# Seven block products instead of eight in the down projection of a feed-forward network

## The chip, the cores and the metric

The kernel is one program on one core of a Trainium2 chip. The metric is the device time of one execution in microseconds (us). The kernel before takes 3278.21 us, the median of three runs from 3277.07 to 3279.9.

The core has TensorE (PE, matmuls), VectorE (DVE), ScalarE (ACT), GpSimd (POOL) and SyncE (SP, whose queue issues the DMAs). Operands lie in SBUF; matmuls write banks of PSUM, 128 partitions by 512 float32.

## The reference

Two transformer blocks on 1024 tokens of width 1024, one after the other, in float32. They hold three feed-forward networks (FFN) of hidden width 2816; these are what matters here:

```python
        up = dwconv3(h @ w_up[l], conv_w[l], conv_b[l])      # first block
        gate, val = jnp.split(up, 2, axis=-1)
        y = (jax.nn.gelu(gate) * val) @ w_down[l]
        x = x + gt_f * rms_norm(y, g_post_ffn[l])
...
def swiglu(x, w_gu, w_down):                                  # second block, twice
    g, u = jnp.split(x @ w_gu, 2, axis=-1)
    return (jax.nn.silu(g) * u) @ w_down
```

The rest (state space and Fourier mixers, two attentions, projections, a last gated layer) is outside the change.

## The kernel before

**Precision.** Every float32 operand is split into a high part (`F32R`, cast by ScalarE, L58) and the remainder (VectorE subtracts, L59). One product is then three matmuls, high x high, high x low, low x high (`mm3`, L96 to L98). `split` is used all over the kernel.

**Up stage of an FFN.** The hidden width is cut into `nff` = 22 tiles of 128. The activation lies transposed and split in `hT`, four tiles with tags `hh` and `hl` of two places each. After two tiles done plainly, the loop over `j` computes each tile with seven block products (`prod`, L296) on sums S1 to S3 of the activation's blocks, which fill the three places of tag `S`. Every finished hidden tile, 128 x 1024, is stored to DRAM (`hidden[j]`, L320 or L246).

**Down stage.** The output, 8 row tiles x 1024, accumulates in SBUF in `yacc` (two places of tag `S`). `load(j)` brings the hidden tile (L357) and 128 rows of `w_down` (L361) into two `raw` places, of which there are three, and splits them: the hidden tile into two places of `b4` (twelve), the weights into `wh` and `wl` (four each). `down` takes two tiles at once: for each of 16 banks six matmuls, then one addition of the bank into `yacc` by VectorE (L377), or for the first pair a copy by ScalarE (L375). Nine such pairs cover 18 tiles. The last four tiles are loaded together and done in one call with 12 matmuls for each bank; behind each row tile `finish` normalises it, adds the residual and prepares the next layer.

**What sets the order.** The program text gives dependencies; a scheduler of the framework then lays out each engine's queue, which runs strictly in that order, and waits between engines are semaphores. Tiles come from pools with a fixed number of places for each tag; a new tile waits until the oldest one's last reader is done. PSUM has six banks under tag `mm` and two under `tp`.

Of the kernel before, what the change touches and what calls it, by code (L numbers as in the profile page):

```python
# [5 lines left out]
F32 = mybir.dt.float32  # L6
F32R = mybir.dt.float32r
I32 = mybir.dt.int32
AF = mybir.ActivationFunctionType
OP = mybir.AluOpType  # L10
PSUM = bass.MemoryType.PSUM
DRAM = bass.MemoryType.DRAM
P = 128
D = 1024
NT = 8
# [4 lines left out]
def f(ap):  # L20
    return ap.bitcast(F32)
# [167 lines left out]
def ffn(k, hT, w_gu, w_down, nff, prep, finish, taps=None, then=None):  # L189
# [5 lines left out]
    nc, v, pool = k.nc, k.nc.vector, k.nc.gpsimd  # L195
    with k.tc.tile_pool(name="ffn", bufs=1) as fp:
        k.places(fp, "b4", 12)
        hidden = k.dr.tile([nff, P, D], F32, name=f"hidden{k.count()}")

        def b4(dt=F32):  # L200
            return fp.tile([P, D], dt, name="b4", tag="b4", bufs=12)

        def big(shape, dt):
            return fp.tile([P] + shape, dt, name="S", tag="S", bufs=3)
# [54 lines left out]
        for a in range(0, 4, 2):  # L259
            c = slice(a, a + 2)  # L260
# [38 lines left out]
        lo, hi = slice(0, 512), slice(512, 1024)  # L299
# [23 lines left out]
        for j in range(2, nff):  # L323
            w = weights(j)
            A, B, C = k.mm(), None, None
# [5 lines left out]
            s, V = b4(), b4()  # L331
            B = k.mm()
# [16 lines left out]
        finish_tile(*prev)  # L349


        ys = [big([4, D], F32) for _ in range(2)]
        yacc = [ys[i // 4][:, i % 4] for i in range(NT)]

        def load(j):
            r = k.raw([P, D])
            nc.sync.dma_start(r, hidden[j])  # L357
            h = b4(F32R), b4(F32R)
            k.split(*h, r)
            r = k.raw([P, D])  # L360
            nc.sync.dma_start(r, w_down[j * P:(j + 1) * P, :])  # L361
            w = k.wide()
            k.split(*w, r)
            return h + w

        def down(ready, first, last):
            for i in range(NT):
                t = slice(i * P, i * P + P)
                for n in range(2):
                    c = slice(n * 512, n * 512 + 512)  # L370
                    po = k.mm()
                    for a, (hh, hl, wh, wl) in enumerate(ready):
                        k.mm3(po, (hh[:, t], hl[:, t]), (wh[:, c], wl[:, c]), a == 0, a == len(ready) - 1)
                    if first:
                        nc.scalar.activation(yacc[i][:, c], po, AF.Copy)  # L375
                    else:
                        v.tensor_tensor(yacc[i][:, c], yacc[i][:, c], po, op=OP.add)  # L377
                if last:
                    finish(fp, i, yacc[i])
                    if i >= 4:  # L380
                        k.flush(2, 1)

        n = nff - 4
        for j in range(0, n, 2):
            down([load(j), load(j + 1)], j == 0, False)
        rows = big([4, D], F32)
        k.rows = [rows[:, a] for a in range(3)]
        k.junk = rows[:, 3]
        prep(fp)
        down([load(j) for j in range(n, nff)], False, True)  # L390
        k.close()
        if then is not None:
            then(fp)
# [10 lines left out]
class Filler:  # L404
# [6 lines left out]
    def add(self, gen):  # L411
        self.jobs.append(gen)
        return gen

    def step(self):
        try:
            return next(self.jobs[0])
        except StopIteration:
            self.jobs.pop(0)
            return 0.0  # L420
# [5 lines left out]
    def finish(self, gen=None):  # L426
        while self.jobs and (gen is None or gen in self.jobs):
            self.step()
# [144 lines left out]
class Mixture:  # L573
# [6 lines left out]
    def put(self, pool, kt, h, src):  # L580
        c = slice(h * 512, h * 512 + 512)
        t = [pool.tile([P, 512], F32R, name=f"mix{a}", tag=f"mix{a}", bufs=2) for a in range(2)]
        self.k.split(t[0], t[1], src)
        for a in range(2):
            self.k.nc.sync.dma_start(self.d[a][kt, :, c], f(t[a]))
# [1283 lines left out]
```

## Time and profile before

| | |
|---|---|
| median of three runs | 3278.21 us |
| the profiled execution | 3276.33 us |
| its span on the core | 3274.3 us |
| TensorE busy | 3088.8 us, 94% |
| VectorE busy | 2133.0 us, 65% |
| ScalarE busy | 1274.7 us, 39% |
| GpSimd busy | 788.9 us, 24% |
| mean granted TensorE clock | 0.976 |

The profile is one execution. Busy times of engines overlap, so they don't add up to the span. In lists of groups a row gives line, engine, operation, out<-in by the program's names with buffer numbers left out (`b` is `b4`), shapes and count, then busy time and mean ns of one, then the idle time ahead of it and what ended it. A matmul's record is longer than the distance to the next one, since they are pipelined; the pace has to be read from starts.

### The profile page before, as it was taken

To read this page: it belongs to the slowest core of one execution; us is meant where nothing else is said; L and a number is where in the kernel's file an instruction comes from. 1 tells how busy PE (TensorE), PEld (TensorE's weight loads), DVE (VectorE), ACT (ScalarE), POOL (GpSimd) and SP (SyncE) were. 2 spreads that over 40 slices of the span, in tenths; PEclk is the share of its full clock that TensorE was granted. 3 is DMA by queue.
4 is the path that set the end of the run, shared out by engine and by line. 5 is a ranking of instruction groups with operands and counts; after the bars stand their busy time and mean duration, and the time that the engine had idled before them with its cause. 6 is when DMAs were issued, how large, how long until landed. Compare 5 with 4: busy or idle time off the path is not lost. (4 is left out here: it accounts for less than half of the span.)

```text
span 3274.3 us, 40844 instructions
## 1 busy us (share of the span) xinstructions
PE 3088.8 (94%) x15362; PEld 2523.1 (77%) x15362; DVE 2133.0 (65%) x3648; ACT 1274.7 (39%) x1975; POOL 788.9 (24%) x903
## 2 busy tenths in 40 slices
PE   5989988899999998999999999999998999999988
PEld 2766767788887878888888878777787788888867
DVE  7766588766666678444446686667677444456686
ACT  3335633444543124333341145446623333341132
POOL 3468525322220014322300020000014222200022
PEclk8999999999999999999999999999998999999999
DMA  7573553122224232222242342111631222242344
GB/s 207 172 223 118 159 175 118 65 90 78 84 90 142 92 129 71 89 78 86 88 141 92 96 142 82 46 45 68 212 129 52 84 77 90 84 148 94 98 144 154
DMA packets 282104, 362.87 MB, mean 111 GB/s; under 512 B 35559, under 2 KB 208871, under 8 KB 281906
## 3 DMA queue, kind: packets, MB, share of 16 engines
q1 hardware_dynamic: 273442, 345.73, 32.7%
q10 hardware_dynamic: 6576, 9.00, 0.8%
q0 software_dynamic: 1888, 5.53, 0.6%
q8 instruction: 121, 1.98, 0.2%
q14 instruction: 77, 0.63, 0.1%
HBM read 274.84 MB, written 91.66 MB: 112 GB/s over the span
## 5 line engine op out<-in xcount | busy, mean ns | idle before, releaser
L296 PE MATMUL mm<-S,wh 128*128 128x512 f32 x1440 | 443.5, 389 | 2.0 <-ACT b L328 2.0
L96 PE MATMUL mm<-wh,b 128*128 128x512 f32 x1056 | 414.3, 393 | 4.0 <-ACT b L58 4.0
L97 PE MATMUL mm<-wl,b 128*128 128x512 f32 x1056 | 413.4, 392 | 0.0
L98 PE MATMUL mm<-wh,b 128*128 128x512 f32 x1056 | 411.9, 391 | 0.0
L377 DVE TENSOR_TENSOR S<-S,mm 128x512 f32<-128x512 f32 x432 | 289.1, 684 | 128.9 <-PE mm L98 128.0
L59 DVE TENSOR_TENSOR wl<-raw,wh 128x1024 fp32r<-128x1024 f32 x242 | 320.3, 1325 | 60.6 <-ACT wh L58 60.4
L58 ACT ACTIVATE wh<-raw 128x1024 fp32r<-128x1024 f32 x244 | 253.4, 1053 | 261.7 <-PE mm L296 140.2
L296 PEld LDWEIGHTS mm<-S,wh 128*128 128x128 f32 x1440 | 270.2, 188 | 58.6 <-ACT b L328 2.4
L96 PE MATMUL mm<-hh,wh 128*128 128x256 f32 (+1 forms) x880 | 300.1, 341 | 15.5 <-ACT hh L58 15.3
L97 PE MATMUL mm<-hl,wh 128*128 128x256 f32 (+1 forms) x880 | 298.9, 340 | 3.5 <-DVE hl L59 3.5
L98 PE MATMUL mm<-hh,wl 128*128 128x256 f32 (+1 forms) x880 | 297.0, 338 | 4.6 <-DVE wl L59 4.6
L296 PE MATMUL mm<-hh,wh 128*128 128x512 f32 x720 | 284.0, 395 | 13.6 <-ACT wh L58 9.8
L296 PE MATMUL mm<-hh,wl 128*128 128x512 f32 x720 | 283.5, 394 | 9.8 <-DVE wl L59 9.8
L296 PE MATMUL mm<-hl,wh 128*128 128x512 f32 x720 | 283.1, 393 | 0.0
L296 PE MATMUL mm<-S,wl 128*128 128x512 f32 x720 | 280.2, 389 | 0.0
L151 POOL TENSOR_TENSOR S<-S 128x1024 f32<-128x1024 f32 x24 | 58.9, 2453 | 802.6 <-ACT S L145 785.9
L343 DVE TENSOR_TENSOR b<-mm,b 128x512 f32<-128x512 f32 x60 | 41.5, 692 | 319.4 <-PE mm L296 314.1
L96 PEld LDWEIGHTS mm<-wh,b 128*128 128x128 f32 x1056 | 199.9, 189 | 45.6 <-ACT b L58 4.5
L97 PEld LDWEIGHTS mm<-wl,b 128*128 128x128 f32 x1056 | 200.0, 189 | 42.5 <-DVE wl L59 0.9
L98 PEld LDWEIGHTS mm<-wh,b 128*128 128x128 f32 x1056 | 199.2, 189 | 42.7 <-DVE b L59 1.2
L58 ACT ACTIVATE b<-raw 128x1024 fp32r<-128x1024 f32 x66 | 69.6, 1059 | 402.1 <-PE mm L97 247.6
L286 POOL TENSOR_TENSOR b<-raw,b 128x512 f32<-128x512 f32 x60 | 79.7, 1329 | 573.8 <-DVE wl L59 573.8
(385 smaller groups left out, 6454.0 us busy)
## 6 DMA issues: line engine op xcount, KB each, us to landing
raw<-in_ffn_w_gu SPq DMA_DIRECT2D x88, 512.0 KB, 3.8
hidden<-b SPq DMA_DIRECT2D x66, 512.0 KB, 2.6
raw<-hidden SPq DMA_DIRECT2D x66, 512.0 KB, 4.5
raw<-in_w_ada SPq DMA_DIRECT2D x48, 512.0 KB, 3.7
raw<-in_w_up SPq DMA_DIRECT2D x44, 512.0 KB, 3.8
raw<-in_ffn_w_down SPq DMA_DIRECT2D x44, 512.0 KB, 4.3
x<-tmp SPq DMA_DIRECT2D x40, 512.0 KB, 2.6
tmp<-x SPq DMA_DIRECT2D x40, 512.0 KB, 5.5
```

Of the source, the lines that this page charges most:

```text
L58: self.nc.scalar.activation(hi, src, AF.Copy)
L59: (eng or self.nc.vector).tensor_tensor(lo, src, f(hi), op=OP.subtract)
L96: mm(out, a[0], b[0], start=start, stop=False)
L97: mm(out, a[0], b[1], start=False, stop=False)
L98: mm(out, a[1], b[0], start=False, stop=stop)
L151: self.nc.gpsimd.tensor_tensor(y, y, row, op=OP.mult)
L286: pool.tensor_tensor(T[:, up], rg[:, dn], T[:, dn], op=OP.subtract)
L296: nc.tensor.matmul(ps, w[y][:, a], x[z][:, a], start=start and a == 0 and n == 0, stop=a == 3 and n == 2, skip_group_check=True)
L343: v.tensor_tensor(V[:, lo], C, X[:, lo], op=OP.add)
L377: v.tensor_tensor(yacc[i][:, c], yacc[i][:, c], po, op=OP.add)
```

## The change

The nine pairs become three groups of three pairs. In a pair the hidden tiles are the operand A (tile j gives A's first half of the inner dimension, tile j+1 the second; tokens 0 to 511 and 512 to 1023 are its other halves), and the weights are B, with two halves of 512 columns. The four blocks of the output come from seven block products, numbered 1 to 7, in the order 1, 2, 5, 3, 6, 7, 4. Each product is done for all three pairs of the group, in four banks, one for 128 tokens: nine matmuls in a bank. Products 1, 6, 7 and 4 accumulate in the same four banks, 5 and 3 share a bank too, and 2 has banks of its own; after each product a bank is added to that part of `yacc` which it belongs to (`collect`). The operands of 1, 2 and 7 are blocks as they are; those of 5, 3, 6 and 4 need sums, which GpSimd makes in place, 24 of 128 x 512 for a group.

`Group` loads six hidden tiles and six weight tiles: a1 into the three `raw` places, b1 into one place of `S`, a2 and b2 into `b4`. `put` splits the operands of one product, in 512 columns each. The split blocks go where the activation lay (`hh`, `hl`, two places each) and into `wh` and `wl`. `step()` prepares the next product's operands ahead in the program text. In the first group, a part of `yacc` is first written by a copy on ScalarE. The last four tiles stay as they were.

```diff
--- before.py
+++ after.py
@@ -349,9 +349,6 @@
...
-        ys = [big([4, D], F32) for _ in range(2)]
-        yacc = [ys[i // 4][:, i % 4] for i in range(NT)]
...
-        def down(ready, first, last):
-            for i in range(NT):
-                t = slice(i * P, i * P + P)
-                for n in range(2):
-                    c = slice(n * 512, n * 512 + 512)
-                    po = k.mm()
-                    for a, (hh, hl, wh, wl) in enumerate(ready):
-                        k.mm3(po, (hh[:, t], hl[:, t]), (wh[:, c], wl[:, c]), a == 0, a == len(ready) - 1)
-                    if first:
-                        nc.scalar.activation(yacc[i][:, c], po, AF.Copy)
...
+        def wblock():
+            tag = ("wh", "wl")[turn["w"] % 2]
+            turn["w"] += 1
+            return k.g.tile([P, D], F32R, name=tag, tag=tag, bufs=k.wbufs)
+        def ablocks():
+            tag = ("hh", "hl")[turn["a"] % 2]
+            turn["a"] += 1
+            return k.g.tile([P, 8, 512], F32R, name=tag, tag=tag, bufs=2).rearrange("p (a b) c -> p a b c", a=4)
+        def bank():
+            turn["s"] += 1
+            if turn["s"] % 2:
+                return k.mm()
+            return k.ps.tile([P, 4, P], F32, name="tp", tag="tp", bufs=2).rearrange("p a b -> p (a b)")
+        class Group:
+            def __init__(self, js):
+                self.js, g = js, len(js)
+                self.b1 = big([4, D], F32)
+                self.a1, self.a2, self.b2 = [], [], []
+                for m, j in enumerate(js):
+                    self.a1.append(k.raw([P, D]))
+                    nc.sync.dma_start(self.a1[m], hidden[j])
+                    nc.sync.dma_start(self.b1[:, m], w_down[j * P:(j + 1) * P, :])
+                for m, j in enumerate(js):
+                    self.a2.append(b4())
+                    nc.sync.dma_start(self.a2[m], hidden[j + 1])
+                    self.b2.append(b4())
+                    nc.sync.dma_start(self.b2[m], w_down[(j + 1) * P:(j + 2) * P, :])
+                self.blocks = {}
+            def put(self, name, a, b):
+                A = ablocks()
+                r = []
+                for m in range(len(self.js)):
+                    x, y = a(m), b(m)
+                    k.split(A[:, m, 0], A[:, m, 1], x)
+                    if m < 2:
+                        B = wblock()
+                        B = B[:, lo], B[:, hi]
                     else:
-                        v.tensor_tensor(yacc[i][:, c], yacc[i][:, c], po, op=OP.add)
-                if last:
-                    finish(fp, i, yacc[i])
-                    if i >= 4:
-                        k.flush(2, 1)
-        n = nff - 4
-        for j in range(0, n, 2):
-            down([load(j), load(j + 1)], j == 0, False)
+                        B = A[:, 3, 0], A[:, 3, 1]
+                    k.split(*B, y)
+                    r.append(((A[:, m, 0], A[:, m, 1]), B))
+                self.blocks[name] = r
+            def prep(self, name):
+                a1, a2, b1, b2 = self.a1, self.a2, [self.b1[:, m] for m in range(len(self.js))], self.b2
+                add = lambda o, x, y: pool.tensor_tensor(o, x, y, op=OP.add)
+                sub = lambda o, x, y: pool.tensor_tensor(o, x, y, op=OP.subtract)
+                if name == 1:
+                    self.put(1, lambda m: a1[m][:, lo], lambda m: b1[m][:, lo])
+                elif name == 2:
+                    self.put(2, lambda m: a2[m][:, lo], lambda m: b2[m][:, lo])
+                elif name == 5:
+                    def s1(m):
+                        t = self.b1[:, 3, lo if m % 2 == 0 else hi]
+                        add(t, a1[m][:, hi], a2[m][:, hi])
+                        return t
+                    def t1(m):
+                        sub(b1[m][:, lo], b1[m][:, hi], b1[m][:, lo])
+                        return b1[m][:, lo]
+                    self.put(5, s1, t1)
+                elif name == 3:
+                    def s4(m):
+                        sub(a1[m][:, hi], a1[m][:, lo], a1[m][:, hi])
+                        sub(a1[m][:, lo], a2[m][:, hi], a1[m][:, hi])
+                        sub(a2[m][:, lo], a2[m][:, lo], a1[m][:, lo])
+                        return a2[m][:, lo]
+                    self.put(3, s4, lambda m: b2[m][:, hi])
+                elif name == 6:
+                    def t2(m):
+                        sub(b1[m][:, hi], b2[m][:, hi], b1[m][:, hi])
+                        sub(b2[m][:, hi], b2[m][:, hi], b1[m][:, lo])
+                        return b2[m][:, hi]
+                    self.put(6, lambda m: a1[m][:, lo], t2)
...
+            def run(self, first, step):
+                def product(po, name, i, start):
+                    t = slice(i * P, i * P + P)
+                    bs = self.blocks[name]
+                    for m, ((ah, al), (bh, bl)) in enumerate(bs):
+                        for z, (x, y) in enumerate(((ah, bh), (ah, bl), (al, bh))):
+                            nc.tensor.matmul(po, x[:, t], y, start=start and m == 0 and z == 0,
+                                             stop=m == len(bs) - 1 and z == 2, skip_group_check=True)
+                def collect(po, i, h, c, new):
+                    y = yacc[i + 4 * h][:, c]
+                    if first and new:
+                        nc.scalar.activation(y, po, AF.Copy)
+                    else:
+                        v.tensor_tensor(y, y, po, op=OP.add)
+                step()
+                U = [k.mm() for _ in range(4)]
+                for i in range(4):
+                    product(U[i], 1, i, True)
+                    collect(U[i], i, 0, lo, True)
+                step()
+                for i in range(4):
+                    po = bank()
+                    product(po, 2, i, True)
+                    collect(po, i, 0, lo, False)
+                step()
+                step()
+                for i in range(4):
+                    po = bank()
+                    product(po, 5, i, True)
+                    collect(po, i, 1, hi, True)
+                    product(po, 3, i, False)
+                    collect(po, i, 0, hi, True)
+                for name, h, c, new in ((6, 0, hi, False), (7, 1, hi, False), (4, 1, lo, True)):
+                    step()
+                    for i in range(4):
+                        product(U[i], name, i, False)
+                        collect(U[i], i, h, c, new)
+        order = (1, 2, 5, 3, 6, 7, 4)
+        groups = [range(j, j + 6, 2) for j in range(0, n, 6)]
+        def preps():
+            for js in groups:
+                gr = Group(js)
+                made.append(gr)
+                for name in order:
+                    gr.prep(name)
+                    yield
+        made = []
+        ahead = preps()
+        next(ahead)
+        ys = [big([4, D], F32) for _ in range(2)]
+        yacc = [ys[i // 4][:, i % 4] for i in range(NT)]
+        for a in range(len(groups)):
+            made[a].run(a == 0, lambda: next(ahead, None))
...
+        ready = [load(j) for j in range(n, nff)]
+        for i in range(NT):
+            t = slice(i * P, i * P + P)
+            for c in (lo, hi):
+                po = k.mm()
+                for a, (hh, hl, wh, wl) in enumerate(ready):
+                    k.mm3(po, (hh[:, t], hl[:, t]), (wh[:, c], wl[:, c]), a == 0, a == len(ready) - 1)
+                v.tensor_tensor(yacc[i][:, c], yacc[i][:, c], po, op=OP.add)
+            finish(fp, i, yacc[i])
...
```

**VectorE, amid the first FFN's down stage.** Before, at the beginning of the third pair (L377 adds a bank to `yacc`, L59 is the subtraction of a split, `b4` and `wl` the low parts of hidden tile and weights):

```order
L377 TENSOR_TENSOR S_8392<-S_8392,mm_8722 128x512 [waits DVE_49,PE_49]
L59 TENSOR_TENSOR wl_8859<-raw_8856,wh_8858 128x1024 [waits DMAHW4_49,Activation_49]
L377 TENSOR_TENSOR S_8392<-S_8392,mm_8730 128x512 [waits DVE_49,PE_49]
L377 TENSOR_TENSOR S_8392<-S_8392,mm_8738 128x512 [waits DVE_49,PE_49]
L59 TENSOR_TENSOR wl_8871<-raw_8868,wh_8870 128x1024 [waits DMAHW6_49,Activation_49]
L377 TENSOR_TENSOR S_8392<-S_8392,mm_8746 128x512 [waits DVE_49,PE_49]
L377 TENSOR_TENSOR S_8392<-S_8392,mm_8754 128x512 [waits DVE_49,PE_49]
L59 TENSOR_TENSOR b4_9017<-raw_9014,b4_9016 128x1024 [waits DMAHW1_49,Activation_49]
```

Now, in the second group, from the first addition of product 1 (L479 is `collect`, tags `hh`, `hl`, `wh` hold the split blocks):

```order
L479 TENSOR_TENSOR S_8429<-S_8429,mm_8889 128x512 [waits PE_49]
L59 TENSOR_TENSOR hh_8998<-b4_8815,hh_8998 128x512 [waits Activation_49]
L59 TENSOR_TENSOR hh_8998<-b4_8817,hh_8998 128x512 [waits Activation_49]
L479 TENSOR_TENSOR S_8429<-S_8429,mm_8890 128x512 [waits PE_49]
L479 TENSOR_TENSOR S_8429<-S_8429,mm_8891 128x512 [waits PE_49]
L59 TENSOR_TENSOR wh_9027<-b4_8809,wh_9027 128x512 [waits Activation_49]
L59 TENSOR_TENSOR wl_9034<-b4_8813,wl_9034 128x512 [waits Activation_49]
L479 TENSOR_TENSOR S_8429<-S_8429,mm_8892 128x512 [waits PE_49]
L59 TENSOR_TENSOR hl_9022<-raw_8798,hl_9022 128x512 [waits Activation_49]
L59 TENSOR_TENSOR hl_9022<-raw_8801,hl_9022 128x512 [waits Activation_49]
L479 TENSOR_TENSOR S_8429<-S_8429,mm_8954 128x512 [waits DVE_49,PE_49]
```

Additions and splits still alternate, but a split has 512 columns instead of 1024, and there are more of them: over a group 42 splits and 28 additions, where three pairs had 12 and 48.

**GpSimd, same group.** Its queue had nothing here in the kernel before. Now it begins like this (L423 an S1 sum into the free fourth part of b1, L424 the differences, in place on a1 in `raw`, b1 in `S`, a2 and b2 in `b4`):

```order
L423 TENSOR_TENSOR S_8797<-raw_8798,b4_8807 128x512 [waits DMAHW7_49,DMAHW1_49,DVE_49]
L424 TENSOR_TENSOR raw_8798<-raw_8798 128x512 [waits Pool_49]
L423 TENSOR_TENSOR S_8797<-raw_8801,b4_8811 128x512 [waits DMAHW3_49,DMAHW0_49]
L424 TENSOR_TENSOR raw_8801<-raw_8801 128x512 [waits Pool_49]
L424 TENSOR_TENSOR S_8797<-S_8797 128x512 [waits DMAHW1_49,DVE_49]
L424 TENSOR_TENSOR S_8797<-b4_8809,S_8797 128x512 [waits DMAHW2_49,Pool_49]
L424 TENSOR_TENSOR raw_8798<-b4_8807,raw_8798 128x512 [waits DVE_49]
L424 TENSOR_TENSOR raw_8801<-b4_8811,raw_8801 128x512 [waits DVE_49]
L424 TENSOR_TENSOR S_8797<-S_8797 128x512 [waits DMAHW2_49,DVE_49]
L424 TENSOR_TENSOR S_8797<-b4_8813,S_8797 128x512 [waits DMAHW4_49,Pool_49]
```

Differences in place wait for the split that reads the old value (`DVE_49`) or for the sum just made (`Pool_49`).

**TensorE, products 5 and 3 of the same group.** Before, every bank was six matmuls and then free for VectorE, and the next bank was another one:

```order
L96 MATMUL mm_8810<-wh_8706,b4_8700 128x512 [waits DVE_49]
L97 MATMUL mm_8810<-wl_8707,b4_8700 128x512
L98 MATMUL mm_8810<-wh_8706,b4_8701 128x512
L96 MATMUL mm_8810<-wh_8718,b4_8712 128x512
L97 MATMUL mm_8810<-wl_8719,b4_8712 128x512
L98 MATMUL mm_8810<-wh_8718,b4_8713 128x512
L96 MATMUL mm_8818<-wh_8706,b4_8700 128x512 [waits DVE_49]
```

Now one bank takes product 5 (operand `hl_8933`), is collected, and then takes product 3 (`hh_8998`):

```order
L471 MATMUL mm_9043<-wh_8938,hl_8933 128x512 [waits DVE_49]
L471 MATMUL mm_9043<-wh_8938,hl_8933 128x512 x2
L471 MATMUL mm_9043<-wl_8945,hl_8933 128x512 x3
L471 MATMUL mm_9043<-hl_8933 128x512 x3
L471 MATMUL tp_9064<-wh_8938,hl_8933 128x512 [waits DVE_49]
L471 MATMUL tp_9064<-wh_8938,hl_8933 128x512 x2
L471 MATMUL tp_9064<-wl_8945,hl_8933 128x512 x3
L471 MATMUL mm_9043<-wh_9004,hh_8998 128x512 [waits DVE_49,Activation_49]
L471 MATMUL mm_9043<-wh_9004,hh_8998 128x512 x2
L471 MATMUL mm_9043<-wl_9012,hh_8998 128x512 [waits Activation_49]
L471 MATMUL mm_9043<-wl_9012,hh_8998 128x512 x2
L471 MATMUL mm_9043<-hh_8998 128x512 [waits Activation_49]
```

Between the last matmul of product 5 in bank `mm_9043` and the first of product 3 the order puts six matmuls of the next bank; the wait for `DVE_49` at product 3's first matmul covers the collection of that bank.

Outside the three down stages the queues of all engines hold the same instructions in the same order as before.

## Rows read from the trace of the kernel before

**Rows 1.** page, span, then busy us (share of span) and instructions per engine
```profile
span 3274.3 us, 40844 instructions
PE 3088.8 (94%) x15362; PEld 2523.1 (77%) x15362; DVE 2133.0 (65%) x3648; ACT 1274.7 (39%) x1975; POOL 788.9 (24%) x903
```

**Rows 2.** stretches: width, busy us (x instructions) per engine, clock, DMA share, GB/s
```profile
core 0: us, PE busy (x) PEld busy (x) DVE busy (x) ACT busy (x) POOL busy (x), PEclk, DMA share, GB/s
980.00:1000.00 20.00, 15.96 (x63) 12.41 (x62) 11.73 (x10) 12.45 (x17) 0.00 (x0) 0.91 0.38 128
1000.00:1020.00 20.00, 20.00 (x89) 16.54 (x89) 11.49 (x14) 11.54 (x16) 0.00 (x0) 1.00 0.74 239
1020.00:1040.00 20.00, 20.00 (x90) 16.57 (x89) 14.93 (x20) 2.96 (x3) 0.00 (x0) 1.00 0.30 93
1680.00:1700.00 20.00, 20.00 (x88) 16.25 (x87) 11.16 (x12) 11.51 (x16) 0.00 (x0) 1.00 0.70 234
2900.00:2920.00 20.00, 20.00 (x89) 16.24 (x88) 10.85 (x11) 11.52 (x15) 0.00 (x0) 1.00 0.60 198
```

**Rows 3.** order of time, ScalarE, second FFN: start us, us, engine, line, [idle <-releaser]
```profile
1704.31 0.60 ACT L375 ACTIVATE S<-mm 128x512 f32<-128x512 f32 x1 [0.76 <-PE mm L98]
1705.67 0.60 ACT L375 ACTIVATE S<-mm 128x512 f32<-128x512 f32 x1 [0.76 <-PE mm L98]
```

**Rows 4.** order of time, VectorE: a split alone, three additions in a row
```profile
961.32 0.68 DVE L59 TENSOR_TENSOR b<-b,b 128x512 fp32r<-128x512 f32 x1
...
1718.37 1.88 DVE L377 TENSOR_TENSOR S<-S,mm 128x512 f32<-128x512 f32 x3
```

**Rows 5.** groups by line: engine, op, shapes, count | busy us, mean ns | idle
```profile
L58 ACT ACTIVATE b<-b 128x512 fp32r<-128x512 f32 x60 | 37.6, 627 | 44.7 <-POOL b L286 44.5
```

**Rows 6.** order of time, GpSimd at 613 us, VectorE idle
```profile
613.35 1.29 POOL L280 TENSOR_TENSOR b<-raw,b 128x512 f32<-128x512 f32 x1
614.59 1.29 POOL L281 TENSOR_TENSOR raw<-raw 128x512 f32<-128x512 f32 x1
```

**Rows 7.** order of time, 1289 to 1296 us, GpSimd, then VectorE
```profile
1289.38 2.16 POOL L280 TENSOR_TENSOR b<-raw,b 128x512 f32<-128x512 f32 x1
1291.49 2.26 POOL L281 TENSOR_TENSOR raw<-raw 128x512 f32<-128x512 f32 x1
...
1292.54 2.30 DVE L265 TENSOR_TENSOR b<-b,b 128x1024 f32<-128x1024 f32 x1
1294.76 1.21 DVE L59 TENSOR_TENSOR S<-b,S 128x1024 fp32r<-128x1024 f32 x1
```

**Rows 8.** order of time, 604 us, GpSimd, then VectorE
```profile
604.83 3.25 POOL L286 TENSOR_TENSOR b<-raw,b 128x512 f32<-128x512 f32 x1 [21.28 <-DVE wl L59]
...
604.60 2.35 DVE L59 TENSOR_TENSOR wl<-raw,wh 128x1024 fp32r<-128x1024 f32 x2
```

**Rows 9.** order of time, 1207 us, GpSimd, then VectorE
```profile
1207.16 2.77 POOL L151 TENSOR_TENSOR S<-S 128x1024 f32<-128x1024 f32 x1 [5.20 <-ACT S L145]
...
1207.84 0.68 DVE L377 TENSOR_TENSOR S<-S,mm 128x512 f32<-128x512 f32 x1
```

**Rows 10.** order of time, TensorE, first FFN, where up ends and down begins
```profile
981.99 0.39 PE L296 MATMUL mm<-hh,b 128*128 128x512 f32 x1
986.42 0.50 PE L96 MATMUL mm<-wh,b 128*128 128x512 f32 x1 [4.04 <-ACT b L58]
...
990.40 0.48 PE L98 MATMUL mm<-wh,b 128*128 128x512 f32 x1
990.72 0.39 PE L96 MATMUL mm<-wh,b 128*128 128x512 f32 x1
```

**Rows 11.** order of time, VectorE, same place: the hidden tile's last multiplication
```profile
990.24 1.22 DVE L319 TENSOR_TENSOR b<-b,b 128x1024 f32<-128x1024 f32 x1
```

**Rows 12.** page, DMA issues: KB each, us to landing
```profile
raw<-hidden SPq DMA_DIRECT2D x66, 512.0 KB, 4.5
```

More of the change, by code (lines that the diff above doesn't have):

```diff
@@ L383, in ffn @@
-        n = nff - 4
-        for j in range(0, n, 2):
-            down([load(j), load(j + 1)], j == 0, False)
+        n = nff - 4
+        lo, hi = slice(0, 512), slice(512, D)
+        turn = {"w": 0, "a": 0, "s": 0}
+        def wblock():
[6 more added lines that the diff above has]
+            return k.g.tile([P, 8, 512], F32R, name=tag, tag=tag, bufs=2).rearrange("p (a b) c -> p a b c", a=4)
@@ new lines, in bank, with t4 @@
+        def bank():
[27 more added lines that the diff above has]
+                        B = B[:, lo], B[:, hi]
+                    else:
+                        B = A[:, 3, 0], A[:, 3, 1]
[32 more added lines that the diff above has]
+                    self.put(6, lambda m: a1[m][:, lo], t2)
+                elif name == 7:
+                    self.put(7, lambda m: a1[m][:, hi], lambda m: b1[m][:, hi])
+                else:
+                    def t4(m):
+                        sub(b2[m][:, lo], b2[m][:, lo], b2[m][:, hi])
+                        return b2[m][:, lo]
+                    self.put(4, lambda m: a2[m][:, hi], t4)
+            def run(self, first, step):
[10 more added lines that the diff above has]
+                        nc.scalar.activation(y, po, AF.Copy)
+                    else:
+                        v.tensor_tensor(y, y, po, op=OP.add)
[22 more added lines that the diff above has]
+                        collect(U[i], i, h, c, new)
@@ L389, in ffn @@
         prep(fp)
-        down([load(j) for j in range(n, nff)], False, True)
+        ready = [load(j) for j in range(n, nff)]
[7 more added lines that the diff above has]
+            finish(fp, i, yacc[i])
+            if i >= 4:
+                k.flush(2, 1)
         k.close()
```

## Prediction

> **What bounds the kernel now.** I read the engines' busy times first, then the busy times by stretch, then the order of instructions in time. TensorE is busy 94% of the span, VectorE 65%, ScalarE 39%, GpSimd 24% [rows 1]. Shares are averages, so the stretches of the down stage count: from 1020 us on each 20 us hold 20.00 us of TensorE at clock 1.00, beside some 14 us of VectorE, 4 us of ScalarE and nothing on GpSimd [rows 2]. The second and third FFN enter the stage without a gap; the first loses time there [rows 2]. So this stage is paid in matmuls, and GpSimd is free in it. The pace: ScalarE copies out one bank per six matmuls, waiting for TensorE each time, and two copies start 1.36 us apart [rows 3]; 1.36/6 = 0.2267 us a matmul.
>
> **The change, part by part.**
>
> *Matmuls removed.* A group of three tile pairs took 3 x 96 = 288 matmuls, 65.3 us. Seven products of four banks of nine matmuls are 252, 57.1 us. Three groups in each of three FFNs: 9 x 36 = 324 fewer, 73.5 us off, if TensorE stays the bound. The last four tiles of each FFN and everything outside the down stage keep their instructions.
>
> *VectorE.* Three pairs had 48 additions into S and 12 splits of 1024 columns. Now a group has 28 additions of 512 columns and 42 splits of 512. Three additions back to back take 1.88 us, so 0.60 us each; a 512-column split takes 0.68 alone [rows 4], and I take 0.60 for it in a row too. 70 x 0.60 = 42.0 us in 57.1. In the first group 16 additions are copies on ScalarE; VectorE has 54 x 0.60 = 32.4 us.
>
> *ScalarE.* 42 casts of 512 columns at 0.627 us [rows 5] are 26.3 us, in a first group 16 copies of 0.60 [rows 3] more, 35.9 us. Both fit under 57.1; no cost where there are tiles to work ahead on, and there are four operand blocks, so that three products, 24 us, can lie prepared.
>
> *GpSimd.* 24 sums of 512 columns per group. Undisturbed they start 1.24 us apart [rows 6]: 29.8 us. That fits too, were it alone. It is not: at 1289 to 1294 us GpSimd's 512-column sums take 2.16 and 2.26 us, and the vector addition of 1024 columns beside them 2.30 instead of 1.21 [rows 7]. They take turns; a collision costs VectorE 1.09 us. At 604.83 it is GpSimd that waits, 3.25 us, while two splits run at full speed [rows 8]. The addition that reads PSUM is spared: 0.68 us inside a GpSimd sum of 2.77 [rows 9]. So the 42 splits, which read two SBUF operands, and the 24 sums exclude each other; the 28 additions from PSUM can hide a sum.
>
> *Time of a group.* Below: were every sum over an addition, 42.0 + 24 x 1.09 - 24 x 0.60 = 53.8 us, and TensorE's 57.1 bounds. Above: nothing hidden, 42.0 + 29.8 = 71.8 us. In the queue additions and splits stand mixed, 28 of 70 are additions, so I let 40% of the collisions be hidden, as if sums came at random: 42.0 + 0.6 x 26.2 = 57.7 us. That is level with TensorE, and two loads that are level do not mesh without loss. Where they touch is the hand-over from product 5 to product 3 in one bank: the order leaves 4 to 6 matmuls (0.9 to 1.4 us) between the end of one and the start of the other, in which the bank must be added up (0.68 us). A split held for 1.09 us ahead of that addition makes it 0.4 to 0.9 us late, and behind it on VectorE stand the next bank's addition and splits. Four hand-overs a group: some 2.3 us. I take 60.0 us for the second and third group, nearest to the random figure, and keep 57.1 and 71.8 as ends. The first group, with 16 additions fewer, has 32.4 + 15.7 = 48.1 us on VectorE and stays TensorE's. Six groups pay 2.9 us each: +17.4 us.
>
> *Start of a stage.* The first group has nothing prepared. Its first product needs b1, which takes a place of the activation's sums S; these are free after their last product, 48 matmuls (10.9 us) before the up stage ends. From then nine loads of 512 KB, 4.7 MB, at the 239 GB/s of the best stretch [rows 2] take 19.7 us, so the last lands 8.8 us after the up stage; product 2 wants it 9.5 us after (one product of 8.2 us, and two thirds of a bank) less 1.3 us for cast and split: late by 0.6 us. At the 128 GB/s of the stretch before it [rows 2] the loads take 36.7 us and are 17 us late. The GpSimd chain is the other clock: the last S1 sum, which product 5 needs 17.7 us after the up stage, stands fourteenth in GpSimd's queue, 17.4 us of sums that may start some 4 us early, longer where splits hold them. In order with it wait the sums of product 3. So between 0 and 17 us; near the rows of 234 to 239 GB/s I take 4 us for the second and third FFN. In the first FFN the vector engine still runs the convolution, and the store of the last hidden tile stands before the last load on SP's queue. There the trace of before already pays: TensorE idles 4.04 us and then starts 11 matmuls in the 4.30 us from 986.42 to 990.72, of which [rows 10] show the first and the last, instead of in 2.49, 5.9 us. The multiplication that ends the tile starts at 990.24 and takes 1.22 us [rows 11], 9.1 us after the up stage's last matmul ended at 982.38 [rows 10]; a load behind that store lands about 4.5 us later [rows 12], 13.6 us, which with 1.3 us is 5.4 us after product 2 wants it. Old and new loss cancel: 0. Together +8 us.
>
> *Elsewhere.* Loads and stores are the same number of bytes. In the later groups the loads of a2 and b2 run ahead, and raw and b1 come free once product 7 is prepared, some 24 us before the next group begins; six loads at 239 GB/s need 13.2 us. No cost. The last four tiles' casts stand among the last group's additions as they did.
>
> *Sum*, on the profiled execution of 3276.33 us (a span of 3274.3 [rows 1] and 2.0 around it): 3276.3 - 73.5 + 17.4 + 8 = 3228.2. The median of the runs lies 1.9 us above that execution: 3230 us.
>
> **A rule to weigh.** The turns in [rows 7] and the wait in [rows 8] show that whoever comes second waits for a whole instruction. The Trainium skill (SBUF — State Buffer, "Who interferes with whom") says the same of a vector instruction with two SBUF inputs against a GpSimd instruction that reads SBUF, calls it an exclusive lock, and leaves the loser to the order of issue; the rows agree. By it nothing but the additions from PSUM could hide a sum, which is the end of 53.8 to 71.8 us already reckoned. Its page "Perfetto Trace Analysis", section "Optimizing Scalar/DVE Operations", goes further: moving work between these two might not help at all. Taken at its word that is rival B below.
>
> **The rivals.**
>
> *A. TensorE stays the bound everywhere.* For it: VectorE has 15 us to spare in a group and prepares three products ahead; two splits in a row can pass a waiting sum [rows 8]. Against: 57.7 us is not below 57.1. Time: 3276.3 - 73.5 + 8 + 1.9 = 3213 us, and with no loss at the starts and the old gap of the first FFN filled some 3199.
>
> *B. The shared port becomes the bound, and the kernel is slower.* The place is VectorE's queue in groups two and three: each sum holds a split, the additions behind it come late, the banks stay full, TensorE waits. At 71.8 us such a group is 6.5 us longer than before; the first group takes 32.4 + 29.8 = 62.2, 3.1 less than before; with 2.7 for the start an FFN gains 12.6 us: 3278.2 + 38 = 3316 us. It decides from about 68 us a group, where 2 x 2.7 equals what the first group, at 57.1, still wins less the start (8.2 - 2.7). TensorE would be busy 80 to 84% there; in the stretch of before with 15.96 of 20 us the granted clock was 0.91 [rows 2], which would add to it. Against: additions and splits are well mixed in the queue, so that nothing hidden is an extreme.
>
> *C. The starts cost what their upper end says.* 17 us in each FFN from late loads or the GpSimd chain, and 60 us a group: 3276.3 - 73.5 + 17.4 + 51 + 1.9 = 3273 us. For it: 12 loads and 24 sums crowd into the first 30 us, and ScalarE's queue mixes product 2's casts with copies that wait for product 1. Against: the up stage's end has the rate of 234 GB/s already in the second FFN [rows 2].
>
> *D. It doesn't do what it says.* 324 matmuls do leave the instruction order, so this has next to no weight.
>
> **How the numbers follow.** Forecast 0.45, A 0.20, C 0.15, B 0.15, the rest 0.05. The forecast's own range is 3213 to 3255. The range down to 3200 takes in A; up to 3285 it takes in C and B's beginning, leaving most of B and a little below A out. What a measurement can tell from no change is about 0.2%, 6.6 us: 3271.7 to 3284.8. Faster than that: the forecast, A, and most of C, 0.77. Within: the rest of C and a mild B, 0.08. Slower: 0.15.
>
> **What would show it.** In the down stage each 252 matmuls should take 57 us in the first group and near 60 in the others, with TensorE 95% busy and clock 1.00. VectorE's splits should show two lengths, 0.68 and up to 1.8 us, GpSimd's sums 1.29 and up to 2.3, the additions from PSUM 0.68 throughout. TensorE's waits should name VectorE's additions at the hand-overs, and loads, splits or casts of product 2 and 5 in the first group. I am wrong if groups two and three run at 57 us (the port is no bound) or above 65 (it is the only bound), or if more than 10 us is idle at a start.

## The result and the profile after

The kernel with the change takes 3308.7 us, the median of four runs (3299.72 to 3314.56), beside 3277.82 us for the kernel before on the same chip. The ratio is 1.0091, interval 1.0067 to 1.0114: 0.9% slower, where 3230 us was forecast and 3285 was the upper end. In the profiled executions the mean granted clock fell from 0.976 to 0.961.

The page of the profiled execution (3314.56 us), the lines that answer to [rows 1]:

```profile
span 3312.8 us, 40565 instructions
PE 3060.1 (92%) x15038; PEld 2479.6 (75%) x15038; DVE 2275.7 (69%) x3738; ACT 1380.9 (42%) x2245; POOL 1129.4 (34%) x1119
```

15038 matmuls instead of 15362 are 324 fewer, as counted. Yet the span is 38.5 us longer (the medians differ by 30.9 us; the profiled execution is the slowest of the four). Next, the stretches of the kernel after, with the columns of [rows 2]. The first nine rows are the nine groups, three for each FFN, each from its first matmul to the next group's first, a third group to the end of its last matmul's record, which is 0.16 us past the start of the next matmul; the width is the second number.

```profile
985.78:1073.62 87.84, 70.08 (x265) 52.93 (x264) 77.89 (x73) 42.40 (x75) 61.76 (x39) 0.88 0.40 148
1073.62:1138.68 65.06, 60.14 (x253) 47.84 (x252) 56.07 (x67) 25.59 (x46) 37.51 (x26) 0.97 0.13 49
1138.68:1200.93 62.25, 58.33 (x254) 47.14 (x253) 49.96 (x66) 21.21 (x31) 12.68 (x8) 1.00 0.41 136
1700.97:1785.82 84.85, 67.03 (x266) 52.00 (x264) 71.10 (x69) 38.48 (x71) 59.49 (x39) 0.88 0.41 146
1785.82:1851.02 65.20, 60.27 (x253) 47.91 (x252) 56.03 (x67) 25.54 (x46) 37.45 (x26) 0.97 0.13 49
1851.02:1914.09 63.07, 59.76 (x254) 48.29 (x253) 49.81 (x66) 21.22 (x31) 12.70 (x8) 0.97 0.41 134
2937.22:3019.16 81.94, 65.41 (x266) 50.82 (x265) 71.59 (x69) 38.48 (x71) 59.80 (x39) 0.90 0.41 150
3019.16:3084.27 65.11, 60.19 (x254) 47.85 (x252) 56.03 (x67) 25.53 (x46) 37.49 (x26) 0.97 0.14 49
3084.27:3146.56 62.29, 58.31 (x254) 47.15 (x253) 49.95 (x66) 21.22 (x31) 12.70 (x8) 1.00 0.39 135
...
1700.00:1720.00 20.00, 13.97 (x59) 10.57 (x58) 20.00 (x14) 7.72 (x14) 19.11 (x12) 0.94 0.76 288
1720.00:1740.00 20.00, 11.98 (x43) 9.13 (x43) 15.75 (x14) 10.27 (x20) 16.69 (x12) 0.72 0.09 36
1740.00:1760.00 20.00, 17.92 (x65) 14.09 (x66) 10.65 (x19) 9.36 (x18) 5.13 (x4) 0.83 0.60 199
1780.00:1800.00 20.00, 20.00 (x90) 16.53 (x89) 19.85 (x19) 8.79 (x16) 16.10 (x10) 1.00 0.00 1
```

Three things are to be seen. First groups are the worst: 82 to 88 us, slower than the 65.3 us of three pairs before. They hold 12 matmuls of the up stage's end besides their 252, so TensorE's own pace would be 57.1 + 12 x 0.2267 = 59.8 us. (The counts in the rows also take in records that overlap an end of the stretch.) Second groups take 65 us and third groups 62 to 63, beside 57.1. And in 1700 to 1720 us VectorE is busy all 20.00 us with only 14 instructions, GpSimd 19.11 with 12: 1.4 and 1.6 us each, for tiles of 512 columns.

VectorE, then GpSimd, in order of time there (start, duration, engine, line; L59 split, L306 a multiplication of the up stage, L423 and L424 the sums, L479 `collect`), answering to [rows 4, 7]:

```profile
1704.09 1.77 DVE L59 TENSOR_TENSOR wh<-b,wh 128x512 fp32r<-128x512 f32 x1
1705.78 1.78 DVE L59 TENSOR_TENSOR wh<-S,wh 128x512 fp32r<-128x512 f32 x1
1707.48 1.78 DVE L59 TENSOR_TENSOR wh<-b,wh 128x512 fp32r<-128x512 f32 x1
1709.19 1.77 DVE L306 TENSOR_TENSOR b<-b,b 128x512 f32<-128x512 f32 x1
...
1740.54 0.67 DVE L479 TENSOR_TENSOR S<-S,mm 128x512 f32<-128x512 f32 x1
1741.14 0.68 DVE L59 TENSOR_TENSOR wl<-b,wl 128x512 fp32r<-128x512 f32 x1
...
1703.57 1.74 POOL L423 TENSOR_TENSOR S<-raw,b 128x512 f32<-128x512 f32 x1
1705.39 1.62 POOL L424 TENSOR_TENSOR raw<-raw 128x512 f32<-128x512 f32 x1
1707.09 1.62 POOL L424 TENSOR_TENSOR raw<-b,raw 128x512 f32<-128x512 f32 x1
1708.67 1.74 POOL L424 TENSOR_TENSOR S<-b,S 128x512 f32<-128x512 f32 x1
```

Both engines start a new instruction every 1.69 us: one on VectorE and one sum in turn, from 1703.6 us to the end of that stretch. From 1739.9 us, with GpSimd idle, VectorE starts an instruction every 0.60 us again. The split pays the 1.09 us of [rows 7]; the sum pays some 0.4 us. This is the exclusive lock that the Trainium skill describes (SBUF — State Buffer, "Who interferes with whom"); the rows agree, but for an overlap of 0.15 us: alone the two would take 0.60 + 1.24 = 1.84 us.

What TensorE waited for in that first group ([idle <-releaser]), and two waits of the second group:

```profile
1716.09 0.73 PE L471 MATMUL mm<-wl,hl 128*128 128x512 f32 x2 [1.99 <-DVE wl L59]
1725.85 0.79 PE L471 MATMUL mm<-hl 128*128 128x512 f32 x1 [9.03 <-ACT hl L58]
1728.24 1.22 PE L471 MATMUL mm<-hl 128*128 128x512 f32 x2 [1.60 <-DVE hl L59]
1742.08 1.65 PE L471 MATMUL mm<-wh,hl 128*128 128x512 f32 x3 [2.65 <-ACT S L477]
...
1802.78 0.96 PE L471 MATMUL mm<-wh,hl 128*128 128x512 f32 x3 [0.48 <-DVE S L479]
1808.88 0.93 PE L471 MATMUL mm<-wh,hh 128*128 128x512 f32 x3 [2.40 <-DVE S L479]
```

And ScalarE's queue ahead of the long one:

```profile
1713.84 0.63 ACT L58 ACTIVATE hh<-S 128x512 fp32r<-128x512 f32 x1 [5.09 <-POOL S L423]
...
1724.64 0.63 ACT L58 ACTIVATE hh<-S 128x512 fp32r<-128x512 f32 x1 [8.65 <-POOL S L423]
1725.18 0.61 ACT L58 ACTIVATE hl<-b 128x512 fp32r<-128x512 f32 x1
```

ScalarE stood 8.65 us at a cast of product 5 (operand in `S`, made by an L423 sum), and the cast of product 2 that TensorE wanted (`hl<-b`) stood behind it. After such waits TensorE goes on at the lower of its two levels (1.2 GHz): three matmuls take 1.65 us at 1742.08 instead of the 0.84 of the three at 1737.68, and 1740 to 1760 us holds 65 matmuls at clock 0.83 where the full stretch at 1780 holds 90.

### The profile page after: what moved, and what is told of

Its sections match the earlier page's. It is cut to its first block, busy times and chain, and to the rows that moved or that the text cites. A ratio compares the mean times of both kernels' runs of the same rounds, so it can differ in the third digit from the quotient of the medians.

```text
span 3312.8 us, 40565 instructions
## 1 busy us (share of the span) xinstructions
PE 3060.1 (92%) x15038; PEld 2479.6 (75%) x15038; DVE 2275.7 (69%) x3738; ACT 1380.9 (42%) x2245; POOL 1129.4 (34%) x1119
## 5 line engine op out<-in xcount | busy, mean ns | idle before, releaser
L296 PEld LDWEIGHTS mm<-S,wh 128*128 128x128 f32 x1440 | 271.0, 188 | 58.6 <-ACT b L328 2.4
L58 ACT ACTIVATE wh<-raw 128x1024 fp32r<-128x1024 f32 x190 | 199.2, 1055 | 258.7 <-PE mm L296 141.5
L59 DVE TENSOR_TENSOR wl<-raw,wh 128x1024 fp32r<-128x1024 f32 x188 | 254.8, 1357 | 43.2 <-ACT wh L58 42.9
L151 POOL TENSOR_TENSOR tmp<-tmp,row 128x1024 f32<-128x1024 f32 x16 | 42.3, 2648 | 580.8 <-DMA raw<-in_ffn_w_gu 443.3
L96 PEld LDWEIGHTS mm<-hh,wh 128*128 128x128 f32 x880 | 172.2, 196 | 33.1 <-ACT hh L58 16.8
L98 PEld LDWEIGHTS mm<-hh,wl 128*128 128x128 f32 x880 | 171.7, 195 | 21.7 <-DVE wl L59 5.4
L97 PEld LDWEIGHTS mm<-hl,wh 128*128 128x128 f32 x880 | 172.1, 196 | 18.4 <-DVE hl L59 4.1
L296 PEld LDWEIGHTS mm<-hh,wh 128*128 128x128 f32 x720 | 137.2, 191 | 43.5 <-ACT wh L58 10.4
L296 PEld LDWEIGHTS mm<-hh,wl 128*128 128x128 f32 x720 | 137.1, 190 | 40.5 <-DVE wl L59 11.8
L277 POOL TENSOR_TENSOR b<-raw 128x512 f32<-128x512 f32 x60 | 81.1, 1352 | 232.6 <-DMA raw<-in_ffn_w_gu 108.9
L296 PE MATMUL mm<-hh,b 128*128 128x512 f32 x480 | 157.9, 390 | 1.7 <-DVE b L347 1.7
L296 PEld LDWEIGHTS mm<-hl,wh 128*128 128x128 f32 x720 | 137.2, 191 | 28.5
```

Source lines behind the costliest of these rows:

```text
L58: self.nc.scalar.activation(hi, src, AF.Copy)
L59: (eng or self.nc.vector).tensor_tensor(lo, src, f(hi), op=OP.subtract)
L96: mm(out, a[0], b[0], start=start, stop=False)
L97: mm(out, a[0], b[1], start=False, stop=False)
L98: mm(out, a[1], b[0], start=False, stop=stop)
L151: self.nc.gpsimd.tensor_tensor(y, y, row, op=OP.mult)
```

## The experiments

The leading theory, P, is the port: VectorE's splits and GpSimd's sums exclude each other and both queues are held. Against it stands Q: operands come late because they wait for sums, and in ScalarE's queue for casts that wait for sums, whoever makes the sums and however fast the splits are. A third, late loads, has the trace against it: 1700 to 1720 us moved 288 GB/s, more than any stretch of [rows 2].

All times are medians; the ratio is to the kernel before on the same chip. That kernel took 3277.82 us beside the kernel after, 3281.39 beside e1 to e4 and 3282.4 beside e5 to e7, so differences in us between kernels of different sets are uncertain by up to some 5 us. Width of the three groups in the second FFN, read from the stretches as above:

| kernel | us | ratio (interval) | groups, us |
|---|---|---|---|
| after | 3308.7 | 1.0091 (1.0067 to 1.0114) | 84.8, 65.2, 63.1 |
| e1, no sums | 3205.09 | 0.9769 (0.9754 to 0.9784) | 60.5, 57.6, 58.1 |
| e2, sums nobody waits for | 3315.74 | 1.0108 (1.0093 to 1.0123) | 78.1, 72.9, 58.6 |
| e3, sums on VectorE | 3202.76 | 0.9759 (0.9743 to 0.9776) | 60.7, 57.2, 57.4 |
| e4, casts in another order | 3299.33 | 1.0055 (1.0040 to 1.0070) | 79.6, 65.2, 62.8 |
| e5, first group on VectorE | 3268.87 | 0.9960 (0.9946 to 0.9974) | 68.6, 65.5, 63.0 |
| e6, later groups on VectorE | 3268.42 | 0.9959 (0.9944 to 0.9975) | 79.6, 57.5, 58.8 |
| e7, half on VectorE | 3272.09 | 0.9972 (0.9962 to 0.9982) | 72.8, 61.0, 63.6 |

**e1: no sums.** In `prep` of the kernel after (the other sums likewise):

```diff
-                add = lambda o, x, y: pool.tensor_tensor(o, x, y, op=OP.add)
-                sub = lambda o, x, y: pool.tensor_tensor(o, x, y, op=OP.subtract)
+                side = lambda x, y: None
...
-                        t = self.b1[:, 3, lo if m % 2 == 0 else hi]
-                        add(t, a1[m][:, hi], a2[m][:, hi])
-                        return t
+                        side(a1[m][:, hi], a2[m][:, hi])
+                        return a1[m][:, hi]
```

> The 24 block sums of each group are left out; products 5, 3, 6 and 4 take unsummed blocks. Theory P (port): GpSimd's sums and VectorE's splits exclude each other, and this makes the first group of each stage 82 to 88 us and the others 63 to 65 instead of 57. Then without sums every split takes 0.68 us, the later groups 57 to 58 us, the first 57 to 62, and the time is 3205 to 3220 us. Theory Q (queue): the first group is late because product 2's casts stand in ScalarE's queue behind casts that wait for sums; without sums that goes too, but the later groups stay at 63 to 65: 3240 to 3255 us. Theory R (neither: late loads, 70 small vector instructions, copies out of banks): groups stay as they are, 3290 us or more.

Measured: 3205.09 us, 103.6 less than after. The three groups of the second FFN:

```profile
1657.08:1717.57 60.49, 60.49 (x265) 49.16 (x264) 43.04 (x70) 39.45 (x72) 0.00 (x0) 1.00 0.56 202
1717.57:1775.21 57.64, 57.64 (x254) 46.99 (x253) 43.34 (x70) 24.72 (x44) 0.00 (x0) 1.00 0.15 55
1775.21:1833.26 58.05, 57.89 (x254) 47.22 (x253) 42.28 (x62) 21.01 (x31) 0.00 (x0) 1.00 0.41 145
```

Splits, casts, loads, banks and the program's order are as in the kernel after, and TensorE's only gap here is 0.16 us, in the third group; at the start there is none. In the first FFN its waits in the down stage add up to 1.9 us. So neither the loads nor the 512-column splits nor the hand-over in one bank cost much by themselves; nearly all of the loss comes with the sums. Whether through the port or through waiting for them, e2 tells.

**e2: the same sums, read by nobody.**

```diff
-                add = lambda o, x, y: pool.tensor_tensor(o, x, y, op=OP.add)
-                sub = lambda o, x, y: pool.tensor_tensor(o, x, y, op=OP.subtract)
+                side = lambda x, y: pool.tensor_tensor(self.b1[:, 3, lo], x, y, op=OP.add)
```

and the calls as in e1.

> GpSimd makes the same 24 sums of the same operands, but into a scratch place that nobody reads; the products take unsummed blocks. Theory P: the port is as contended as before, splits beside sums take 1.7 us and the later groups stay at 61 to 65 us; only the chain sum, cast, split is gone from the first group: 3250 to 3285 us. If it is the waiting for sums and not the port (dependency), the time is that of the kernel without sums, 3205 to 3220 us. Theory R: 3290 us or more.

Measured: 3315.74 us, no better than after. The groups of the second FFN:

```profile
1705.36:1783.50 78.14, 64.54 (x266) 50.11 (x264) 77.50 (x68) 39.57 (x72) 66.23 (x42) 0.93 0.42 158
1783.50:1856.37 72.87, 64.16 (x254) 49.64 (x253) 64.94 (x72) 24.73 (x44) 48.27 (x31) 0.93 0.12 44
1856.37:1914.99 58.62, 57.91 (x254) 47.22 (x253) 42.69 (x63) 21.11 (x31) 0.00 (x0) 1.00 0.43 144
```

Here no cast waits for a sum, and the loss is back. GpSimd ran ahead, so that the first two stretches hold all the sums and the third none; the third has nearly e1's time, and the second, with 31 GpSimd instructions, takes 72.87. For 68 instructions VectorE needs 77.50 us where 70 took 43.04 in e1. So the port brings the whole loss without anyone waiting for a sum. The time lies above P's own range of 3250 to 3285 us all the same, where R was expected, which e1 had ruled out: the expectation took off what the waiting costs and did not reckon with sums that wait for nothing crowding into two groups. How much of the first group's loss in the kernel after goes through late sums, such as the one that held a cast for 8.65 us there, this does not separate.

**e3: the sums on VectorE.**

```diff
-                add = lambda o, x, y: pool.tensor_tensor(o, x, y, op=OP.add)
-                sub = lambda o, x, y: pool.tensor_tensor(o, x, y, op=OP.subtract)
+                add = lambda o, x, y: v.tensor_tensor(o, x, y, op=OP.add)
+                sub = lambda o, x, y: v.tensor_tensor(o, x, y, op=OP.subtract)
```

> The sums are made by VectorE instead of GpSimd, nothing else is changed. Theory P: a sum costs VectorE 0.60 us of its own instead of up to 1.09 us of waiting, no split is longer than 0.69 us; 94 x 0.60 = 56.4 us a group against 57.1 of TensorE, so the later groups take 58 to 62 us and the first one 65 to 70: 3225 to 3260 us. If VectorE's load is what counts and not the port, 24 instructions more make it slower than the changed kernel: 3310 us or more.

Measured: 3202.76 us, faster than all expectations and than both kernels: 2.4% below the kernel before. Its page, the second FFN's groups, and three rows of VectorE's order:

```profile
PE 3025.8 (94%) x15038; PEld 2466.5 (77%) x15038; DVE 2241.0 (70%) x3954; ACT 1381.9 (43%) x2245; POOL 786.5 (25%) x903
```

```profile
1663.56:1724.30 60.74, 60.63 (x265) 49.14 (x264) 60.39 (x100) 39.88 (x72) 0.00 (x0) 1.00 0.53 202
1724.30:1781.47 57.17, 57.17 (x253) 47.29 (x252) 56.33 (x94) 24.93 (x44) 0.00 (x0) 1.00 0.16 56
1781.47:1838.89 57.42, 57.42 (x254) 47.38 (x253) 51.79 (x79) 21.37 (x31) 0.00 (x0) 1.00 0.39 126
```

```profile
1738.55 0.68 DVE L424 TENSOR_TENSOR S<-b,S 128x512 f32<-128x512 f32 x1
1739.15 0.68 DVE L479 TENSOR_TENSOR S<-S,mm 128x512 f32<-128x512 f32 x1
1739.75 0.69 DVE L424 TENSOR_TENSOR b<-b,S 128x512 f32<-128x512 f32 x1
```

VectorE has 216 instructions more than in the kernel after and is busy 34.7 us less. The products wait for the same sums as in the kernel after, and in this FFN nothing is late. That speaks against Q too, though not by itself: the sums also come sooner here, 0.60 us each instead of one in 1.69. VectorE is busy 56.33 of 57.17 us in the second group and TensorE doesn't wait for it at all.

**e4: product 5's casts behind product 2's.** The tenable part of Q was the 9.03 us wait at a cast that stood behind another. In the first group the casts of product 5 and later go behind product 2's last one:

```diff
-        self.nc.scalar.activation(hi, src, AF.Copy)
+        self.cast = self.nc.scalar.activation(hi, src, AF.Copy)
...
                 for name in order:
-                    gr.prep(name)
+                    if name not in (1, 2) and js is groups[0]:
+                        with k.tc.issue_after(last.ins):
+                            gr.prep(name)
+                    else:
+                        gr.prep(name)
+                        last = k.cast
```

> As the changed kernel, sums on GpSimd, but in the first group of each stage the casts of product 5 and later stand in ScalarE's queue behind those of product 2. Theory Q: TensorE's waits of 5.6 to 9.0 us for the cast of product 2 go, with the slow clock behind them: 10 us less per stage, 3275 to 3285 us. Theory P: the wait moves to product 5, whose last sum comes at the same time or later, since the chain of sums and splits through the port sets it: 3295 to 3310 us.

Measured: 3299.33 us, 9.4 less than after, with intervals that just touch. TensorE's longest waits in the second FFN's first group:

```profile
1719.00 1.62 PE L471 MATMUL mm<-wh,hh 128*128 128x512 f32 x3 [6.45 <-DVE S L479]
1727.58 1.65 PE L471 MATMUL mm<-wh,hl 128*128 128x512 f32 x3 [2.77 <-ACT S L477]
```

The 9.03 us wait for `hl` is gone and one of 6.45 us for a bank has come in its place. In the first FFN the wait moved to the next products instead: there the longest is 8.62 us, for a cast that waited for a sum. By the medians the queue's order is about a tenth of the loss (9.4 of 105.9 us over e3); for the rest it decides where the loss shows.

**e5 and e6: where the sums cost.** e5 puts the first group's sums on VectorE and leaves the later ones on GpSimd; e6 is the reverse (`!= 0`).

```diff
-                add = lambda o, x, y: pool.tensor_tensor(o, x, y, op=OP.add)
-                sub = lambda o, x, y: pool.tensor_tensor(o, x, y, op=OP.subtract)
+                eng = v if self.js[0] == 0 else pool
+                add = lambda o, x, y: eng.tensor_tensor(o, x, y, op=OP.add)
+                sub = lambda o, x, y: eng.tensor_tensor(o, x, y, op=OP.subtract)
```

> Sums on VectorE in the first group of each stage, on GpSimd in the second and third. If the first group's loss is its own (nothing prepared, 24 sums and 42 splits through one port, 14 more sums of the next group in the same stretch), the first group falls from 82 to 88 us to 62 to 68 and the later ones stay at 63 to 65: 3243 to 3258 us. If what the first group wins comes back later, since its speed only moves the crowding, 3285 us or more.

> The other way round: sums on GpSimd in the first group, on VectorE in the second and third. Port: the later groups take 57 to 59 us, and the first one, which no longer has the second group's GpSimd sums in its stretch, 74 to 82: 3243 to 3270 us. If only the start matters (queue order, late loads), the later groups' gain is small: 3290 us or more.

Measured: 3268.87 and 3268.42 us. e6 came as expected, e5 above what was expected. Over e3, e6's 72 sums on GpSimd cost 65.7 us, 0.91 each, near the whole 1.09 of a collision; e5's 144 cost 66.1, 0.46 each. The two add up to 131.8 us, while all 216 together cost 105.9. So the two losses are not simply added, and 0.91 and 0.46 are averages and no fixed prices. In e5 the first group is not free of sums either: in its stretch of the second FFN lie 16 of the next group's, and it takes 68.6 us. In the profiled execution, 3276.38 us and the slowest of five, the largest single loss is one wait in the first FFN's second group, which is 77.5 us long there; whether the other four have it isn't known:

```profile
1076.43 1.65 PE L472 MATMUL mm<-wh,hl 128*128 128x512 f32 x3 [12.13 <-DVE S L480]
```

**e7: half the sums.** S1 and S4 on VectorE, the weights' three on GpSimd, twelve and twelve in a group:

```diff
...
-                        add(t, a1[m][:, hi], a2[m][:, hi])
+                        add(v, t, a1[m][:, hi], a2[m][:, hi])
...
-                        sub(b1[m][:, lo], b1[m][:, hi], b1[m][:, lo])
+                        sub(pool, b1[m][:, lo], b1[m][:, hi], b1[m][:, lo])
...
```

> Half a dose: the sums of the hidden tiles (S1, S4: 4 a pair) on VectorE, those of the weights (4 a pair) on GpSimd. If each collision has its price, half of the sums cost half: 3250 to 3260 us. If the additions from PSUM can hide a dozen sums a group, as the forecast reckoned for 40% of them, the later groups take 57 to 58.5 us and the first 66 to 72: 3215 to 3235 us.

Measured: 3272.09 us, missed by both expectations. 108 sums on GpSimd cost 69.3 us over e3, two thirds of the loss of 216. By the averages of e6 and e5, 36 x 0.91 + 72 x 0.46 = 65.9; since the two don't add up, that this comes near may be luck. Even a few collisions cost: in its third group only six sums lie, and TensorE still loses 6.2 us over e3 (the group's stretch, then TensorE's order of time):

```profile
1817.63:1881.26 63.63, 59.63 (x254) 48.40 (x253) 50.36 (x69) 21.25 (x32) 9.53 (x6) 0.97 0.39 132
```

```profile
1835.77 0.93 PE L471 MATMUL mm<-wh,hh 128*128 128x512 f32 x3 [1.66 <-ACT hl L58]
1841.77 0.93 PE L471 MATMUL mm<-wh,hl 128*128 128x512 f32 x3 [2.34 <-DVE S L479]
```

The six sums run from 1821.07 to 1831.5 us. The waits come after them, while VectorE works off what was held, and the group's mean granted clock is 0.97.

## Why the prediction was wrong

| term | forecast | measured |
|---|---|---|
| 324 matmuls fewer | -73.5 | -73.5 (e3's groups: 57.2 and 57.4) |
| six later groups over 57.1 | +17.4 | +40.4 |
| starts, less the old loss of 5.9 | +8 | +69.3 |
| sum | -48.1 | +36.2 (the span: +38.5) |

The measured terms are the nine widths less 57.1, for first groups less 59.8. The remaining 2.3 us of the span lie outside the three stages and were not traced.

**Right.** The matmuls and their price. That the loads would bring no great loss: e1, with the same loads, loses hardly any time at the starts. The cost of one collision, 1.09 us, and that the additions from PSUM are spared: L479 takes 0.67 us in the rows above. That e3 comes out at 3202.76 us, which by its ratio of 0.9759 is 3199 us on the forecast's base and rival A's lower end, says that with the port out of the way the price of the matmuls holds.

**The step that failed first: "The first group, with 16 additions fewer, has 32.4 + 15.7 = 48.1 us on VectorE and stays TensorE's."** It was reckoned as a steady load, with the 40% of hidden collisions of a full group, and only the group's own 24 sums. In fact 39 sums and 69 VectorE instructions lie in the stretch, since the next group's first 16 sums are made ahead in it (one of its own is made before), and VectorE is busy 71 to 78 us. In 1700 to 1720 us splits and sums simply alternate, with hardly an instruction from PSUM to hide a sum; that the 16 additions given to ScalarE are missing there is argued and not tested. And nothing lies prepared, so held splits and late sums become waits of TensorE: in the rows above 1.99 and 1.60 us end with a split, and 9.03 us with a cast behind one that waited for a sum. The start had been reckoned from GpSimd's chain too, at 0 to 17 us and "longer where splits hold them", and taken at 4; the first groups lost 22 to 28. Of the 24.1 us over e3's first group in the second FFN, 17.7 are idle time (84.85 - 67.03 less 0.11 in e3), and 6.4 are matmuls at the lower clock level behind it (67.03 - 60.63). The text's own sign of being wrong, more than 10 us idle at a start, was passed, and the second groups, at 65.1 to 65.2 us, stand just past its other one of 65.

**The second: "I let 40% of the collisions be hidden, as if sums came at random."** They come in bursts: as soon as an operand is free GpSimd makes all the sums it can, 10 in 1780 to 1800 us, where VectorE is busy 19.85 us with 19 instructions. Over a whole second group VectorE is busy 56.03 of 65.20 us, so the mean fitted as reckoned (57.7); but the collections stand behind the held splits and TensorE waits while the backlog is worked off. e3 has the same busy time, 56.33 us, evenly spread, and loses nothing. So "two loads that are level do not mesh without loss" was wrong for level loads and too mild for bursts: 8 and 5 to 6 us a group, not 2.9. The upper end of 71.8 us was not consistent with the text's own price either: 42.0 + 24 x 1.09 is 68.2.

**The rivals.** B named the cause, the port, but looked for it in groups two and three, where it costs 40 us, and let the first group gain 3.1 us, where it costs most; that its 3316 us lies near the measured time is luck. C named the place, the start, and put it down to late loads, GpSimd's chain or a mixed queue; e1 rules out the loads, e4 gives the queue about a tenth, and the chain is slow because of the port: a sum in 1.69 us instead of 1.24. Neither priced the clock, which B only named: in the second FFN the matmuls behind the waits cost 6.4 + 3.1 + 2.3 = 11.8 of the 37.8 us over e3, by the differences of TensorE's busy time.

**The rule.** That moving work between these two engines might not help (the Trainium skill, Perfetto Trace Analysis, "Optimizing Scalar/DVE Operations") was weighed in with 0.15 as rival B. Here it did worse than not help: the same sums cost 105.9 us more on GpSimd than on VectorE (3308.7 to 3202.76).

## What to carry to other kernels

Before work is moved to an idle GpSimd, compare what it takes on VectorE (0.60 us here) with what its collision takes from VectorE (1.09 us): where VectorE is busy with instructions that read two SBUF operands, the offloading can cost more than it removes, as it did here. On VectorE the 24 sums of a group just fitted, 94 x 0.60 = 56.4 us beside 57.1 of TensorE. Add up such loads per stretch and not per stage, first of all where nothing is prepared, and count what is made ahead for the next group in the stretch in which it is made. An engine that is 98% busy with short instructions can be harmless (second group of e3), while one at 86% with held ones stops the rest (second group of the kernel after).

## What was not expected of the hardware

With work in both queues, from 1703.6 to 1720 us, VectorE and GpSimd took turns, instruction by instruction, at 1.69 us for a split and a sum of 512 columns, while alone their starts lie 0.60 and 1.24 us apart, 1.84 together; GpSimd's sums rose from 1.29 to 1.62 and 1.74 us, VectorE's splits from 0.68 to 1.78. That is no fixed rule: in [rows 8] two splits pass a waiting sum. VectorE at 56.33 of 57.17 us, with a sum, a split or an addition from PSUM every 0.60 us, kept TensorE at 57.17 us for 252 matmuls. And a wait costs more than its length: with 17.8 us of idle time in the first group the granted clock averaged 0.88 in its 85 us, and TensorE was busy 6.4 us longer than in e3 for the same matmuls.
